# Side work of the attention heads moved between ticks, and one pair of weights turned on TensorE, in a two-layer trunk

## The chip, the cores and the metric

One core of a Trainium2 chip runs the whole program. The metric is the device time of one execution in microseconds (us); before the change it is the median of three runs. The engines are named as the profile names them: PE (TensorE's matmuls), PEld (its weight loads), DVE (VectorE), ACT (ScalarE), POOL (GpSimd) and SP (SyncE, which here only issues DMAs).

## The reference, cut to what matters

Two layers over 256 tokens of width 2048, batch 1, all in float32:

```python
h = rmsnorm(x, norm0); qa,ka,va,iq,ik,iw,qb,kb,vb,gate = split(h @ w_in0)
# A: 10 heads, one shared key/value; an indexer picks 64 causal keys for each query
# B: 6 heads, a mixture of three dilated windows
x = x + (concat(o_a, o_b) * silu(gate)) @ w_out0
h = rmsnorm(x, norm1); qc,kc,vc,qd,kd,vd,fl,gate = split(h @ w_in1)
# C: 8 heads, stick-breaking:
#    w = exp(log_sigmoid(z) + tail), tail = reverse cumulative sum of log_sigmoid(-z)
# D: 8 heads, softmax with forget gates: logits + c[t] - c[s], c = cumsum(log f)
x = x + (concat(o_c, o_d) * silu(gate)) @ w_out1
return rmsnorm(x, norm_f)
```

## The kernel before

**Projections.** The four weight matrices are read as 39 *jobs*, most of them 512 columns wide: 14 for layer 0's input (B0, K, I0, I1, B1 to B3, A0, A2, A4, A6, A8, B4, B5; an A job holds two heads, a *pair*), P0 to P3 for its output, 17 for layer 1's input (C0, F1, G1, C2 to C7, D0 to D7), Q0 to Q3 for its output. A job runs over 16 k-tiles; at each, `project` (L323, L324, L326) issues six matmuls: weights split into a high and a low part (`whi`, `wlo`), tokens likewise, three products for each of two token tiles.

**The split.** Weights arrive as `raw` tiles of four k-tiles (three buffers, DMAs on SP's queue, `load`). `split` halves each: ACT copies `whi` (L282), DVE subtracts `wlo` (L283). It is issued for two k-tiles at a time and runs three of these halves ahead of the matmuls; `whi` and `wlo` have four buffers each.

**Side work.** When a job ends, its head starts as a Python generator. Each k-tile of a full-width job is one *tick* (six matmuls); at each tick `advance` resumes the generators that are due, the oldest first. `yield n` means n ticks later. So the order of every engine's instructions is written out by these numbers: what a head issues at a tick stands in ACT's, DVE's, PE's and SP's queues behind what was issued before and ahead of the next split. A new head starts every 16 ticks, and a head lives 23 to 43 ticks, so two or three heads overlap.

**A head.** A transpose goes by DVE inside 32x32 blocks (`grid`, L428), a store to DRAM (`fard`, L437 or L511) and a read back (L448; in four pieces for the weights, L442); near the end of a layer TensorE does it (`turn`, L400). A C head, in ticks from its start:

- 0: scaled q and k (L866, L867), their `grid`; in `vg1` the value (L487, L490) and the gate u = g * sigmoid(g): ACT's Exp (L877), DVE's add, reciprocal (L882) and product (L887)
- 2 store and 6 read of q and k; 8 `grid` of u, 10 store, 14 read (`gate_late`)
- 10: q and k cut into parts (L408 to L410); 14: scores on PE, z (L936), ACT's Abs, Exp, Ln, Relu (L939 to L942)
- 20: scan (L945), z minus sum (L947), Exp (L948); 22 `grid`, 24 store, 28 read
- 38: the weights cut into parts (`cut`, L477, L478, tiles `ph`, `pl`); 43: matmuls with the value into the one PSUM tile `o` (`weigh_out`, L464 to L466, L531), times the gate (L532), into the parts `yh`, `yl` of the output

A D head runs `softmax_head`: cut of q and k at 10, scores and softmax at 14 (L549, L551), shares (L565) and `grid` at 16, store 18, read 22, cut 26, out 29; its u is turned by `gate_turned` (grid 4, store 6, read 10). D6 and D7 turn on TensorE. A pair of A heads (`heads_a`): rotated q and both gates (L769) at 0, q cut at 12, softmax of the first head at 16, share, `grid` 18, store 20, read 24; the second four ticks later; cuts at 28 and 36 (tiles `pA`, `pB`), out at 39, with the product at L809. All pairs, A8 too, go through DRAM. B4 and B5 turn on TensorE.

All these stores and reads, and the `raw` loads, are issued in order from SP's queue: an issue that waits (for a `grid`, for a store to land, for a free `raw` tile) holds all behind it.

Of the kernel before, what the change touches and what calls it, by code (L numbers as in the profile page):

```python
# [14 lines left out]
P = 128  # L15
# [159 lines left out]
def trunk(ctx, tc, x, xT, g1, w0, wo0, w1, wo1, bf, gf, consts, rope, out):  # L175
# [66 lines left out]
    def load():  # L242
        i = st["load"]
        if i == len(pieces):
            return
        st["load"] += 1
        wd, off, n, w = pieces[i]
        if i < len(FIRST):

            kt = sum(FIRST[:i])  # L250
            raws[i] = home[kt // 8][:, (kt % 8) * w:(kt % 8 + n) * w]
        else:
            raws[i] = wp.tile([P, n * w], F32, name="raw", tag="raw")
        if i == 1 or 3 < i < len(FIRST):
            load_xT(kt)
        nc.sync.dma_start(raws[i], wd[off:off + P * n * w].rearrange("(p f) -> p f", p=P))
        if i in (0, 2):
            load_xT(i)
        if i == len(FIRST) + 1:
            for th in range(NT):  # L260
                for c0, c1 in ((0, D),):
                    nc.sync.dma_start(xs[:, th, c0:c1], x[th * P:(th + 1) * P, c0:c1])
            nc.sync.dma_start(rt.rearrange("p a b -> p (a b)"), rope)
        if i == len(FIRST) + 2:
            nc.sync.dma_start(cons, consts)
# [231 lines left out]
    def gate_turned(u):  # L497
        uT = hp.tile([P, SEQ], F32, name="uT", tag="uT")
        start(far([u], uT, 4, 2, 4))
        return arrived(uT, NT)  # L500

    def gate_late(u, n=NT):

        box = []

        def way():
            yield 8
            t = grid([u])
            d = dr.tile([P, P * n], F32, name="fard", tag=f"fard{n}", bufs=4)
            yield 2  # L510
            nc.sync.dma_start(d, t)  # L511
            yield 4
            uT = hp.tile([P, P * n], F32, name="uT", tag="uT" if n == NT else "rl")
            read_back(uT, d, n)
            box.append(arrived(uT, n))

        start(way())
        return box
# [57 lines left out]
        yield 2 if last else ticks  # L576
        weigh_out(ph, pl, p1, v, uT[0] if isinstance(uT, list) else uT, kt)

    def softmax_head(qk, ticks, nb, v, u, rs, kt, last, near):

        uT = u if last else gate_turned(u)
        qk = yield from qk_turned(qk, ticks, last)
        pr, l = soft(qk, nb() if callable(nb) else nb)
        if not last:
            yield 2
        share(pr, factor(l, rs))
        if near:
            yield 4
            blocks = quarters(turn([pr[:, 0:P], pr[:, P:SEQ], pr[:, SEQ:384]]))
        else:  # L590
            yield from moved(grid([pr]), pr, 2, 4, True)
            yield 4
            blocks = arrived(pr, 3)
        yield from weights_out(blocks, v, uT, kt, last)

# [164 lines left out]
    def heads_a(ps, h):  # L760
        qk = hp.tile([P, 512], F32, name="qk", tag="qk")
        u = hp.tile([P, 2, NT, P], F32, name="u2", tag="u2", bufs=1)
        tgs = {}
        for th in range(NT):
            rotate(qk[:, th * 256:(th + 1) * 256], ps[th][:, 0:256], rt[:, th, 0:P], rt[:, th, 256:384], 2, P)
            tgs[1 - th] = hp.tile([P, 256], F32, name="tg", tag="tg")
            nc.scalar.activation(tgs[1 - th], ps[1 - th][:, 256:512], AF.Tanh, scale=hr0[:, 1 - th:2 - th])
        for th in (1, 0):
            nc.vector.scalar_tensor_tensor(u[:, :, th, :], tgs[th].rearrange("p (a b) -> p a b", a=2), 1.0,  # L769
                                           ps[th][:, 256:512].rearrange("p (a b) -> p a b", a=2),  # L770
                                           op0=OP.add, op1=OP.mult)
        uT = gate_late(u.rearrange("p a b c -> p (a b c)"), 4)
        yield from far([qk], qk, 2, 2, 4)
        yield 4
        q = arrived(qk, 4)
        f = hp.tile([P, 256], F32, name="qqf", tag="qkf", bufs=1)
        hi = hp.tile([P, 256], F32R, name="qqh", tag="qkh", bufs=1)
        lo = hp.tile([P, 256], F32R, name="qql", tag="qkl", bufs=1)
        nc.scalar.activation(quarters(hi), q[:, 2:4], AF.Copy)
        nc.scalar.activation(quarters(f), q[:, 0:2], AF.Copy)  # L780
        nc.vector.tensor_tensor(quarters(lo), q[:, 2:4], quarters(hi).bitcast(F32), op=OP.subtract)
        yield 4
        js = [slice(j * P, (j + 1) * P) for j in range(2)]
        away = []
        for j in range(2):
            pr, l = soft((f[:, js[j]], kA, hi[:, js[j]], lo[:, js[j]], kAh, kAl), nbA)
            yield 2
            share(pr, factor(l, hr0))

            t = hp.tile([P, 512], F32, name="far", tag=("ih2", "il2")[j], bufs=1)[:, 0:384]  # L790
            start(moved(grid([pr], t), t, 2, 4, True))
            away.append(arrived(t, 3))
            yield 2
        yield 4

        ph, pl = (hp.tile([P, 2, SEQ], F32R, name="pA" + n, tag="i" + n, bufs=1) for n in "hl")
        p1h, p1l = (hp.tile([P, 2 * P], F32R, name="pB" + n, tag=t, bufs=1) for n, t in (("h", "y"), ("l", "sp")))
        for j in range(2):
            cut((quarters(ph[:, j, :]), quarters(pl[:, j, :])), away[j][:, 0:2])
            cut((quarters(p1h[:, js[j]]), quarters(p1l[:, js[j]])), away[j][:, 2:3])  # L800
            yield (8, 3)[j]
        uT, = uT
        po = pa.tile([P, 512], F32, name="o", tag="o", bufs=1)
        vh, vl = vAs
        flat = lambda t: t.rearrange("p a b -> p (a b)")
        three_of(po, vh[:, 0], vl[:, 0], flat(ph), flat(pl), True, False)
        o1 = po.rearrange("p (a b c) -> p a b c", a=2, b=2)[:, :, 1, :]
        three_of(o1, vh[:, 1], vl[:, 1], p1h, p1l, False, True)
        nc.vector.tensor_tensor(uT, quarters(po), uT, op=OP.mult)  # L809
        kt = YPOS[f"A{h}"]  # L810
        cut([quarters(flat(t[:, kt:kt + 2, :])) for t in ys], uT)
# [55 lines left out]
            nc.vector.tensor_scalar(qk[:, k], ps[th][:, P:256], r1[:, th:th + 1], None, op0=OP.mult)  # L867
        return qk

    def vg1(ps, o, apart=False, third=False):  # L870

        u = hp.tile([P, SEQ], F32, name="u", tag="u")
        e = hp.tile([P, SEQ], F32, name="e", tag="tg")
        v, upper, lower = values(ps, o, r1, (), third)
        for th in range(NT):
            t = slice(th * P, (th + 1) * P)
            nc.scalar.activation(e[:, t], ps[th][:, o + P:o + 256], AF.Exp, scale=nr1[:, th:th + 1])  # L877
            upper(th)
        if apart:
            yield 1  # L880
        nc.vector.tensor_scalar(e, e, 1.0, 3.0e38, op0=OP.add, op1=OP.min)
        nc.vector.reciprocal(e, e)  # L882
        if apart:
            yield 1
        for th in range(NT):
            t = slice(th * P, (th + 1) * P)
            nc.vector.scalar_tensor_tensor(u[:, t], ps[th][:, o + P:o + 256], r1[:, th:th + 1], e[:, t],  # L887
                                           op0=OP.mult, op1=OP.mult)
        lower()
        return v, u  # L890

    def forget(ps):
# [36 lines left out]

    def stick(qk, ticks, v, u, kt):  # L930

        uT = gate_late(u)
        qk = yield from qk_turned(qk, ticks, 0)
        pZ = scores(qk)
        z = hp.tile([P, 384], F32, name="z", tag="sn")
# [2 lines left out]
        zp = hp.tile([P, 384], F32, name="zp", tag="ih", bufs=1)  # L938
        nc.scalar.activation(sp, z, AF.Abs)  # L939
        nc.scalar.activation(sp, sp, AF.Exp, scale=-1.0)  # L940
        nc.scalar.activation(sp, sp, AF.Ln, bias=1.0)
        nc.scalar.activation(zp, z, AF.Relu)  # L942
        yield 6
        for _, s in BLK:
            nc.vector.tensor_tensor_scan(sp[:, s][:, ::-1], sp[:, s][:, ::-1], zp[:, s][:, ::-1], 0.0,  # L945
                                         op0=OP.add, op1=OP.add)
# [1 line left out]
        nc.scalar.activation(z, z, AF.Exp)  # L948
        yield 2
        yield from moved(grid([z]), z, 2, 4, True)  # L950
        yield 10
        yield from weights_out(arrived(z, 3), v, uT, kt, 0, 5)

    def head_c(ps, h):
        qk = scaled_qk(ps, 0, (0, 3), (1, 2))
        start(moved(grid([qk]), qk, 2, 4))
        v, u = yield from vg1(ps, 256, h == 0, h % 3 == 2)
        yield from stick(qk, 10 if h else 8, v, u, h)

# [12 lines left out]

    def tail(ps, c2):
# [123 lines left out]
```

## Time and profile before

| | |
|---|---|
| median of 3 runs | 898.07 us (895.04 to 900.7) |
| the profiled execution | 896.82 us |
| its span, first to last instruction | 894.7 us |
| PE, PEld busy | 879.1 us (98%), 734.5 us (82%) |
| DVE, ACT, POOL busy | 659.0 us (74%), 475.3 us (53%), 50.2 us (6%) |
| granted TensorE clock, mean | 0.997 of full speed |

Busy times are sums over the profiled execution; a matmul's duration overlaps the next one's, so a busy PE is not a PE at its full rate. The step from one matmul's start to the next one's shows the rate. A row of a timeline shows the start, the duration, the instruction, and in brackets the engine's idle time before it and what ended it. `out<-in` are names of tiles.

### The profile page before, as it was taken

What the parts mean: (1) busy time and instruction counts of PE and PEld (TensorE: products, weight loads), DVE (VectorE), ACT (ScalarE), POOL (GpSimd) and SP (SyncE); (2) the same over time, 40 slices, a digit from 0 to 9 for tenths busy, and PEclk for the clock granted to TensorE, in tenths of its full rate; (3) what the DMA queues carried; (4) which work ended last, traced back from release to release, by engine and by line L of the source; (5) the groups of instructions that cost most, each with busy time, mean ns of one, the idle gap of its engine ahead of it and who ended that gap; (6) DMA issues with size and microseconds to landing.
All of it is one profiled execution on the core that took longest, in us unless ns stands there. A gap on an engine that the chain in (4) does not pass through costs nothing.

```text
span 894.7 us, 12055 instructions
## 1 busy us (share of the span) xinstructions
PE 879.1 (98%) x4185; PEld 734.5 (82%) x4185; DVE 659.0 (74%) x1162; ACT 475.3 (53%) x840; POOL 50.2 (6%) x69
## 2 busy tenths in 40 slices
PE   9999999999999999999999999999999999999996
PEld 6988888888888877888898888888777888888886
DVE  7587888877777777666667777777787777776563
ACT  7644555454454555555455555555555555555440
POOL 0013100000000000000000000000010000001110
PEclk9999999999999999999999999999999999999998
DMA  9887555676777765766486756666685776665542
GB/s 360 316 314 268 209 204 192 209 265 208 258 247 234 228 219 210 277 229 243 146 287 222 254 202 238 217 231 224 231 281 202 268 236 244 236 219 182 192 185 95
DMA packets 89661, 207.59 MB, mean 232 GB/s; under 512 B 32112, under 2 KB 60800, under 8 KB 71424
## 3 DMA queue, kind: packets, MB, share of 16 engines
q1 hardware_dynamic: 88128, 203.52, 64.7%
q0 software_dynamic: 896, 2.12, 0.8%
q10 hardware_dynamic: 576, 1.19, 0.4%
q8 instruction: 33, 0.54, 0.2%
q14 instruction: 28, 0.23, 0.1%
HBM read 185.29 MB, written 21.50 MB: 231 GB/s over the span
## 4 chain that ended last, share of the span: by engine, by line
PE 79%; DVE 8%; DMA 6%; issue 3%; ACT 3%; SPq 1%; POOL 0%; DVEq 0%; POOLq 0%; ACTq 0%
PE pj L323 25%; PE pj L324 25%; PE pj L326 25%; DVE wlo L283 3%; DMA raw<-in_w_out_dram 2%; DMA qk<-fard 2%; ACT whi L282 2%; DMA raw<-in_w_in_dram 1%; DMA fard<-far 1%; DVE far L428 1%; DVE e L882 1%; PE s L538 1%; PE o L531 0%; PE s L465 0%; PE s L466 0%
## 5 line engine op out<-in xcount | busy, mean ns | idle before, releaser
L283 DVE TENSOR_TENSOR wlo<-raw,whi 128x1024 fp32r<-128x1024 f32 (+3 forms) x300 | 352.6, 1189 | 149.7 <-ACT whi L282 148.2
L323 PE MATMUL pj<-whi,xh 128*128 128x512 f32 (+3 forms) x992 | 378.5, 383 | 0.0
L324 PE MATMUL pj<-whi,xl 128*128 128x512 f32 (+3 forms) x992 | 376.4, 381 | 0.0
L282 ACT ACTIVATE whi<-raw 128x1024 fp32r<-128x1024 f32 (+3 forms) x300 | 299.8, 1025 | 123.6 <-PE pj L324 73.4
L326 PE MATMUL pj<-wlo,xh 128*128 128x512 f32 (+3 forms) x992 | 297.3, 381 | 1.9 <-DVE wlo L283 1.8
L326 PEld LDWEIGHTS pj<-wlo,xh 128*128 128x128 f32 x992 | 182.9, 188 | 39.8 <-DVE wlo L283 4.5
L323 PEld LDWEIGHTS pj<-whi,xh 128*128 128x128 f32 x992 | 186.7, 188 | 34.0 <-ACT whi L282 1.3
L324 PEld LDWEIGHTS pj<-whi,xl 128*128 128x128 f32 x992 | 186.6, 188 | 33.0
L323 PE MATMUL pj<-whi,yh 128*128 128x512 f32 (+1 forms) x248 | 95.7, 386 | 0.0
L324 PE MATMUL pj<-whi,yl 128*128 128x512 f32 (+1 forms) x248 | 94.9, 383 | 0.0
L326 PE MATMUL pj<-wlo,yh 128*128 128x512 f32 (+1 forms) x248 | 76.7, 382 | 0.0
L326 PEld LDWEIGHTS pj<-wlo,yh 128*128 128x128 f32 x248 | 46.6, 188 | 9.2
L324 PEld LDWEIGHTS pj<-whi,yl 128*128 128x128 f32 x248 | 46.7, 188 | 8.7
L323 PEld LDWEIGHTS pj<-whi,yh 128*128 128x128 f32 x248 | 46.6, 188 | 8.6
L477 ACT ACTIVATE yh<-uT 128x256 fp32r<-128x256 f32 (+1 forms) x27 | 12.4, 458 | 61.1 <-DVE uT L532 45.2
L551 ACT ACTIVATE sn<-sn,nm 128x128 f32<-128x128 f32 (+1 forms) x48 | 21.5, 449 | 35.2 <-DVE nm L549 35.2
L598 ACT ACTIVATE sq<-xs 128x512 f32<-128x512 f32 x23 | 14.3, 623 | 30.2 <-DVE xs L821 26.5
L882 DVE RECIPROCAL e<-e 128x256 f32<-128x256 f32 x16 | 28.1, 1753 | 0.6
L382 POOL TENSOR_TENSOR qk<-rot,rot 128x256 f32<-128x256 f32 x16 | 11.9, 741 | 230.3 <-ACT sn L551 109.7
L948 ACT ACTIVATE z<-z 128x384 f32<-128x384 f32 x8 | 4.2, 526 | 38.0 <-DVE z L947 38.0
L877 ACT ACTIVATE e<-pj,nr 128x128 f32<-128x128 f32 x32 | 11.8, 367 | 21.9 <-DVE qk L867 21.9
L478 DVE TENSOR_TENSOR yl<-uT,yh 128x256 fp32r<-128x256 f32 (+1 forms) x27 | 12.8, 475 | 14.3 <-ACT yh L477 14.3
(216 smaller groups left out, 715.0 us busy)
## 6 DMA issues: line engine op xcount, KB each, us to landing
raw<-in_w_in_dram SPq DMA_DIRECT2D x108, 1024.0 KB, 6.1
raw<-in_w_out_dram SPq DMA_DIRECT2D x32, 1024.0 KB, 4.9
fard<-far SPq DMA_DIRECT2D x43, 256.0 KB, 2.1
qk<-fard SPq DMA_DIRECT2D x25, 256.0 KB, 5.2
fard<-far SPq DMA_DIRECT2D x28, 192.0 KB, 2.0
raw<-in_w_in_dram SPq DMA_DIRECT2D x4, 672.0 KB, 10.0
fard<-far SPq DMA_DIRECT2D x20, 128.0 KB, 4.6
uT<-fard SPq DMA_DIRECT2D x20, 128.0 KB, 4.2
```

The lines of the kernel that those rows point to most:

```text
L282: nc.scalar.activation(hi, rw, AF.Copy)
L283: nc.vector.tensor_tensor(lo, rw, hi.bitcast(F32), op=OP.subtract)
L323: nc.tensor.matmul(o, a, wh, start=(kt == 0), stop=False)
L324: nc.tensor.matmul(o, b, wh, start=False, stop=False)
L326: nc.tensor.matmul(o, a, wl, start=False, stop=(kt == KT - 1))
L382: nc.gpsimd.tensor_tensor(dst, t1[:, 0:n], t2[:, 0:n], op=OP.add)
L477: nc.scalar.activation(dst[0], src, AF.Copy)
L478: nc.vector.tensor_tensor(dst[1], src, dst[0].bitcast(F32), op=OP.subtract)
L551: nc.scalar.activation(sn[:, s], sn[:, s], AF.Exp, scale=-1.0, bias=nm[:, th:th + 1], accum_out=l[:, th:th + 1])
L598: nc.scalar.activation(j, xs[:, th, c * 512:(c + 1) * 512], AF.Square, accum_out=ss[:, i, th, c:c + 1])
L877: nc.scalar.activation(e[:, t], ps[th][:, o + P:o + 256], AF.Exp, scale=nr1[:, th:th + 1])
L882: nc.vector.reciprocal(e, e)
```

## The change

1. `stick`: after Abs and Exp of z four ticks pass before Ln and Relu, then four (instead of six) to the scan. The weights' `grid`, store and read come two ticks later (24, 26, 30), the cut is at 38 as before.
2. `vg1`: the value's low part first; add and reciprocal two ticks later, the product two ticks after that, now for all C and D heads but D7 (C0 had it with one tick each). The later `yield`s are cut by four, so that q and k are cut at tick 10 as before. C heads' u is turned at the same ticks as before; D heads' u by `gate_late` (grid 8, store 10, read 14).
3. `heads_a`: u is formed at tick 4; the pair's store, read, first cut come two ticks later (22, 26, 30 for the first head; store 26, read 30 for the second), the second cut stays at 36, out at 40. The cut weights get rooms named afresh.
4. The last pair (A8, `near`) turns its weights on TensorE: six `turn` matmuls, no store and read; its cuts are at 21 and 24, out at 27 instead of 39.
5. `softmax_head(behind)`: D0's cut comes four ticks later (30, out 33).
6. `load`: x is read in four DMAs instead of two.

```diff
-                for c0, c1 in ((0, D),):
+                for c0, c1 in ((0, 1024), (1024, D)):
                     nc.sync.dma_start(xs[:, th, c0:c1], x[th * P:(th + 1) * P, c0:c1])
...
-    def gate_late(u, n=NT):
+    def gate_late(u, first=8, n=NT):
...
-            yield 8
+            yield first
             t = grid([u])
...
-        uT = u if last else gate_turned(u)
+        uT = u if last else gate_late(u, 4) if rs is None else gate_turned(u)
...
             yield from moved(grid([pr]), pr, 2, 4, True)
-            yield 4
+            yield 8 if behind else 4
...
 def heads_a
+        start(far([qk], qk, 2, 2, 4))
+        yield 4
         for th in (1, 0):
             nc.vector.scalar_tensor_tensor(u[:, :, th, :], ...
-        uT = gate_late(u.rearrange("p a b c -> p (a b c)"), 4)
-        yield from far([qk], qk, 2, 2, 4)
-        yield 4
+        uT = gate_late(u.rearrange("p a b c -> p (a b c)"), 4, 4)
+        yield 8
...
+        near = h == HA - 2
+        if near:
+            sm = []
+            for j in range(2):
+                sm.append(scored(j))
+                yield 2
+                share(sm[j][0], factor(sm[j][1], hr0))
+            yield 1
+            ph, pl, p1h, p1l = rooms(("ih2", "il2"), ("ph", "pl"))
+            for j in range(2):
+                pr = sm[j][0]
+                turned(j, quarters(turn([pr[:, 0:P], pr[:, P:SEQ], pr[:, SEQ:384]])))
+                yield 3
+        else:
...
-            start(moved(grid([pr], t), t, 2, 4, True))
+                start(moved(grid([pr], t), t, 4, 4, True))
...
-        yield 4
-        for j in range(2):
-            cut(...)
-            yield (8, 3)[j]
+            yield 6
+            ph, pl, p1h, p1l = rooms(("ih", "il"), ("y", "sp"))
+            turned(0, away[0])
+            yield 6
+            turned(1, away[1])
+            yield 4
...
 def vg1
+        lower()
         if apart:
-            yield 1
+            yield 2
         nc.vector.tensor_scalar(e, e, 1.0, 3.0e38, op0=OP.add, op1=OP.min)
         nc.vector.reciprocal(e, e)
         if apart:
-            yield 1
+            yield 2
...
-        lower()
         return v, u
...
 def stick
-        uT = gate_late(u)
+        uT = gate_late(u, 4)
...
         nc.scalar.activation(sp, sp, AF.Exp, scale=-1.0)
+        yield 4
         nc.scalar.activation(sp, sp, AF.Ln, bias=1.0)
         nc.scalar.activation(zp, z, AF.Relu)
-        yield 6
+        yield 4
...
         yield from moved(grid([z]), z, 2, 4, True)
-        yield 10
+        yield 8
...
-        v, u = yield from vg1(ps, 256, h == 0, h % 3 == 2)
-        yield from stick(qk, 10 if h else 8, v, u, h)
+        v, u = yield from vg1(ps, 256, True, h % 3 == 2)
+        yield from stick(qk, 6, v, u, h)
...
-        v, u = yield from vg1(ps, 256, third=h == 0)
-        yield from softmax_head(qk, 10, lambda: biases[h], v, u, None, HC + h, last, h >= HDD - 2)
+        v, u = yield from vg1(ps, 256, not last, h == 0)
+        yield from softmax_head(qk, 6, lambda: biases[h], v, u, None, HC + h, last, h >= HDD - 2, h == 0)
```

## Rows read from the trace of the kernel before

**Rows 1.** The page's first lines: the span, and busy time, share of the span and instructions of each engine.

```profile
span 894.7 us, 12055 instructions
...
PE 879.1 (98%) x4185; PEld 734.5 (82%) x4185; DVE 659.0 (74%) x1162; ACT 475.3 (53%) x840; POOL 50.2 (6%) x69
```

**Rows 2.** Busy time of each engine, with the count of instructions, in windows that reach from a job's first projection matmul to the next job's (columns: window, its length, PE, PEld, DVE, ACT, POOL, granted clock, DMA share, GB/s). In order: jobs D3, C6, C7, D0, D1, D2, then A8, B4 and B5.

```profile
678.09:701.05 22.96, 22.96 (x108) 19.17 (x107) 18.29 (x32) 12.32 (x23) 1.83 (x3) 1.00 0.76 259
...
560.73:584.05 23.32, 23.27 (x107) 19.09 (x106) 17.73 (x26) 13.23 (x25) 0.00 (x0) 1.00 0.66 225
584.05:607.55 23.50, 23.29 (x108) 19.09 (x106) 17.73 (x26) 13.41 (x25) 0.00 (x0) 1.00 0.68 238
607.55:631.03 23.48, 23.27 (x107) 19.08 (x106) 17.97 (x28) 13.19 (x24) 0.72 (x1) 1.00 0.64 214
631.03:655.20 24.17, 23.29 (x107) 19.08 (x106) 18.77 (x31) 13.59 (x25) 1.83 (x3) 1.00 0.67 230
655.20:681.70 26.50, 24.15 (x112) 19.59 (x111) 19.18 (x36) 14.39 (x31) 0.71 (x1) 1.00 0.74 252
254.30:278.30 24.00, 24.00 (x114) 20.08 (x113) 19.28 (x41) 12.44 (x25) 1.49 (x2) 1.00 0.73 235
278.30:303.06 24.76, 24.27 (x114) 20.02 (x113) 18.92 (x42) 12.89 (x25) 1.48 (x2) 1.00 0.73 235
303.06:328.70 25.64, 24.54 (x115) 20.02 (x113) 19.17 (x43) 13.29 (x27) 1.48 (x2) 1.00 0.74 247
```

**Rows 3.** Timeline of PE in job D1, two matmuls in succession at k-tile 6.

```profile
639.87 0.39 PE L324 MATMUL pj<-whi,xl 128*128 128x512 f32 x1
641.14 0.73 PE L326 MATMUL pj<-wlo,xh 128*128 128x512 f32 x2 [0.88 <-DVE wlo L283]
```

**Rows 4.** Timeline of DVE in job C6, from the start of the head before it (C5) to that head's predecessor's scan.

```profile
564.54 0.61 DVE L867 TENSOR_SCALAR qk<-pj,rstd 128x128 f32<-128x128 f32 x2
565.18 0.71 DVE L428 STREAM_TRANSPOSE far<-qk 128x512 f32<-128x512 f32 x1
565.84 0.29 DVE L881 TENSOR_SCALAR e<-e 128x256 f32<-128x256 f32 x1
566.16 1.75 DVE L882 RECIPROCAL e<-e 128x256 f32<-128x256 f32 x1
567.95 0.61 DVE L887 SCALAR_TENSOR_TENSOR u<-pj,rstd,e 128x128 f32<-128x128 f32 x2
568.48 0.34 DVE L490 SCALAR_TENSOR_TENSOR v<-pj,rstd,v 128x128 fp32r<-128x128 f32 x1
568.74 2.35 DVE L283 TENSOR_TENSOR wlo<-raw,whi 128x1024 fp32r<-128x1024 f32 x2
571.00 1.00 DVE L945 TENSOR_TENSOR_SCAN sp<-sp,zp 128x128 f32<-128x128 f32 x2
```

**Rows 5.** Timeline of ACT in the same stretch.

```profile
561.48 0.53 ACT L941 ACTIVATE sp<-sp 128x384 f32<-128x384 f32 x1
561.91 0.51 ACT L942 ACTIVATE zp<-z 128x384 f32<-128x384 f32 x1
...
572.63 0.52 ACT L948 ACTIVATE z<-z 128x384 f32<-128x384 f32 x1 [4.67 <-DVE z L947]
573.06 1.04 ACT L282 ACTIVATE whi<-raw 128x1024 fp32r<-128x1024 f32 x1
```

**Rows 6.** Timeline of PE in job D2: C7's matmuls into `o`, the projection matmul behind them, and, two ticks later, the first of D0's into `o`.

```profile
671.02 0.28 PE L464 MATMUL o<-ph,v 128*128 128x256 f32 x1
...
671.51 0.48 PE L323 MATMUL pj<-whi,xh 128*128 128x512 f32 x1
...
676.35 0.36 PE L464 MATMUL o<-ph,v 128*128 128x256 f32 x1 [1.82 <-DVE uT L532]
```

**Rows 7.** Timeline of PE in jobs B4 and B5: the second matmul of the out of the pairs A4 and A6.

```profile
289.31 0.50 PE L465 MATMUL o<-pAl,vAh 128*128 128x512 f32 x1 [0.49 <-DVE pAl L478]
...
314.94 0.50 PE L465 MATMUL o<-pAl,vAh 128*128 128x512 f32 x1 [1.07 <-DVE pAl L478]
```

**Rows 8.** Timeline of PE in job P0, where B5's head turns its q and k on TensorE and makes its scores.

```profile
335.63 0.44 PE L400 MATMUL tp<-cons,qk 128*128 128x128 f32 x2 [0.72 <-POOL qk L380]
...
339.46 0.49 PE L538 MATMUL s<-qkf 128*128 128x128 f32 x2 [0.30 <-ACT qkf L409]
...
340.57 0.39 PE L465 MATMUL s<-qkl,qkh 128*128 128x256 f32 x1 [0.50 <-DVE qkl L410]
```

**Rows 9.** SP's queue in job B5 (start, time of the issues, what is issued): the read of A8's first weights, and a `raw` load.

```profile
322.49 1.74 SPq L442 DMA_DIRECT2D far<-fard  x4
324.33 0.39 SPq L256 DMA_DIRECT2D raw<-in_w_out_dram  x1
```

**Rows 10.** Timeline of PE in job Q0: D6's three transposes on TensorE and the projection matmuls behind them.

```profile
802.44 0.49 PE L400 MATMUL tp<-cons,sn 128*128 128x128 f32 x3
802.68 0.48 PE L323 MATMUL pj<-whi,yh 128*128 128x512 f32 x1
803.00 0.39 PE L324 MATMUL pj<-whi,yl 128*128 128x512 f32 x1
```

**Rows 11.** SP's queue near the start: the loads of x.

```profile
14.81 0.94 SPq L262 DMA_DIRECT2D xs<-in_x_dram  x2
```

**Rows 12.** The page's DMA issues: the stores of turned weights (count, KB each, median us from issue to landing).

```profile
fard<-far SPq DMA_DIRECT2D x28, 192.0 KB, 2.0
```

More of the change, by code (lines that the diff above doesn't have):

```diff
@@ L577, in weights_out, with softmax_head @@
         weigh_out(ph, pl, p1, v, uT[0] if isinstance(uT, list) else uT, kt)
-    def softmax_head(qk, ticks, nb, v, u, rs, kt, last, near):
-        uT = u if last else gate_turned(u)
+    def softmax_head(qk, ticks, nb, v, u, rs, kt, last, near, behind=False):
+        uT = u if last else gate_late(u, 4) if rs is None else gate_turned(u)
         qk = yield from qk_turned(qk, ticks, last)
@@ L783, in heads_a @@
         js = [slice(j * P, (j + 1) * P) for j in range(2)]
-        away = []
-        for j in range(2):
[L786 to L790, printed above, removed]
-            start(moved(grid([pr], t), t, 2, 4, True))
-            away.append(arrived(t, 3))
-            yield 2
-        yield 4
-        ph, pl = (hp.tile([P, 2, SEQ], F32R, name="pA" + n, tag="i" + n, bufs=1) for n in "hl")
@@ L797, in heads_a, with rooms @@
[L797 to L800, printed above, removed]
-            yield (8, 3)[j]
+        near = h == HA - 2
+        scored = lambda j: soft((f[:, js[j]], kA, hi[:, js[j]], lo[:, js[j]], kAh, kAl), nbA)
+        def rooms(a, b):
+            return ([hp.tile([P, 2, SEQ], F32R, name="pA" + n, tag=t, bufs=1) for n, t in zip("hl", a)]
+                    + [hp.tile([P, 2 * P], F32R, name="pB" + n, tag=t, bufs=1) for n, t in zip("hl", b)])
@@ new lines, in turned @@
+        def turned(j, pt):
+            cut((quarters(ph[:, j, :]), quarters(pl[:, j, :])), pt[:, 0:2])
+            cut((quarters(p1h[:, js[j]]), quarters(p1l[:, js[j]])), pt[:, 2:3])
+        if near:
[11 more added lines that the diff above has]
+        else:
+            away = []
+            for j in range(2):
+                pr, l = scored(j)
+                yield 2
+                share(pr, factor(l, hr0))
+                t = hp.tile([P, 512], F32, name="far", tag=("ih2", "il2")[j], bufs=1)[:, 0:384]
+                start(moved(grid([pr], t), t, 4, 4, True))
+                away.append(arrived(t, 3))
+                yield 2
[5 more added lines that the diff above has]
+            yield 4
@@ L868, in scaled_qk, with vg1 @@
         return qk
-    def vg1(ps, o, apart=False, third=False):
+    def vg1(ps, o, apart=True, third=False):
         u = hp.tile([P, SEQ], F32, name="u", tag="u")
@@ L878, in vg1 @@
             upper(th)
+        lower()
         if apart:
-            yield 1
+            yield 2
         nc.vector.tensor_scalar(e, e, 1.0, 3.0e38, op0=OP.add, op1=OP.min)
@@ L883, in vg1 @@
         if apart:
-            yield 1
+            yield 2
         for th in range(NT):
@@ L956, in head_c @@
         start(moved(grid([qk]), qk, 2, 4))
-        v, u = yield from vg1(ps, 256, h == 0, h % 3 == 2)
-        yield from stick(qk, 10 if h else 8, v, u, h)
+        v, u = yield from vg1(ps, 256, True, h % 3 == 2)
+        yield from stick(qk, 6, v, u, h)
     def head_cf(ps, qk):
         v, u = yield from vg1(ps, 0)
-        yield from stick(qk, 10, v, u, 1)
+        yield from stick(qk, 6, v, u, 1)
     def head_d(ps, h):
```

## The prediction, made before the changed kernel was run

> **What bounds the kernel now.** The page comes first: PE is busy 98% of the span, DVE 74%, ACT 53% [rows 1]. That says that PE sets the end, not that it runs at its full rate, for a busy matmul can stand in the array while the next one waits. So the second view is a table by job: windows from a job's first projection matmul to the next job's. The reader is to see that the windows differ although the jobs are alike. D3 takes 22.96 us, PE is busy all of it at clock 1.00, and D4 to D6 repeat that length; this is a slot in which PE waits for nothing. C6, C7, D0, D1 and D2 hold the same projections and take 23.32, 23.50, 23.48, 24.17 and 26.50 [rows 2]. A8 with its pair's extra matmuls takes 24.00 without a wait, B4 and B5 with as many matmuls 24.76 and 25.64 [rows 2]. Only this excess can be won by moving side work: the matmuls themselves stay.
>
> The third view, PE's timeline, tells what the excess waits for. In D1 the low product of k-tile 6 stands 1.27 us behind the one before it, 0.88 of it idle until DVE's `wlo` [rows 3]. DVE's own timeline shows why `wlo` is late: at a head's start it works off scaled k, `grid`, add, reciprocal, product and the value's low part, from 564.54 to 568.74, before it comes to the split [rows 4]. In D2 the wait is another: D0's matmuls into the single tile `o` wait 1.82 for DVE's product on C7's `o`, two ticks earlier [rows 6]. In B4 and B5 the outs of pairs A4 and A6 wait 0.49 and 1.07 for the second head's low part [rows 7]. In P0 PE waits 0.72, 0.30 and 0.50 for B5's rotated and cut q and k [rows 8]. Behind this lies SP's queue: a `raw` load at 324.33 is issued only after the four reads of A8's weights, which took the queue from 322.49 [rows 9].
>
> **The change, part by part.**
>
> *`vg1` and `stick` (the wlo waits).* Excess over 22.96: 0.36 (C6) + 0.54 (C7) + 0.52 (D0) + 1.21 (D1) = 2.63. In D2 it is 3.54; there two outs fall into one slot, and an out costs PE 0.49 (671.02 to 671.51) [rows 6], so 3.05 is waiting: 1.82 at `o`, the other 1.23 mostly `wlo`. The change takes add, reciprocal and product (0.29 + 1.75 + 0.61 = 2.65) out of the cluster ahead of k-tile 6's `wlo` [rows 4]; the longest of these waits in the slots is 1.21, so it goes with a margin of over 1 us. What is late next? Now 0.29 + 1.75 = 2.04 stands ahead of k-tile 8's `wlo`. Before, both `wlo` ended at 571.09; after, by the same durations, 568.74 - 2.65 + 1.18 + 2.04 + 1.18 = 570.49: no later. On ACT, Ln and Relu (0.53 + 0.51) [rows 5] no longer stand ahead of a split at tick 14, but at tick 18, when a new head's Exps have just gone; same work, smaller lump. z's Exp, for which ACT now idles 4.67 ahead of k-tile 10's `whi` [rows 5], comes two ticks later, ahead of k-tile 12's; DVE is then less behind, so that wait shrinks. I take the whole of it: -2.63 and -1.23. Bounds: 0, if the lump only moves, and -3.86.
>
> *D0 four ticks later (`behind`).* Its matmuls come six ticks after C7's instead of two. Two ticks are 2 x 22.96/16 = 2.9 us, and they missed by 1.82 [rows 2, 6], so six are enough: -1.82. What hides the delay is that D0's output is read only in Q0, five slots on.
>
> *The pairs.* B4 0.76 + B5 1.64 over A8's 24.00 [rows 2]. Out at 40 leaves four ticks instead of three behind the second cut: 1.4 us more against waits of 0.49 and 1.07 [rows 7]. Stores come two ticks later, so that they are issued when their `grid` is done and don't hold the `raw` loads in SP's queue. -2.40; bounds 0 and -2.40.
>
> *The last pair on TensorE.* Removed from SP: two stores and eight reads (a set of four takes 1.74 of the queue [rows 9]), on which `raw` loads of P0 wait. Added on PE: six transposes. Three took 802.44 to 803.00 with the first matmul behind them [rows 10], of which a matmul's own step is about 0.23 (a slot of 22.96 over some 96 projections and 12 smaller matmuls): 0.33, twice 0.66. ACT and DVE do the same cuts, from PSUM. The waits in P0, 0.72 + 0.30 + 0.50 = 1.52 [rows 8], should shrink since A8's second cut no longer stands ahead of B5's q and k on ACT, and `raw` is earlier; I take half, -0.76, for the rotation there is not touched. Bounds 0 and -1.52.
> For a 128x128 transpose the Trainium skill (TensorE: Matmul & The Clock Gate, Part 4: PE-mode transpose) has about 275 ns in a kernel's context. By that the six would cost 1.65 and the sum below would be 1.0 smaller; the trace here has 0.33 for three.
>
> *The rest.* Gates of D heads are stored and read four ticks later, z's store and reads two ticks later: as many DMAs as before, on the same queue. z's store now meets the gate's store (tick 10 of the next head), its four reads the gate's read (14), and the `raw` loads of tick 16 stand behind them. Weights are read at 30 and cut at 38: eight ticks, 11.5 us. x in four pieces adds two issues, 0.47 each [rows 11], where SP then waits for `raw` buffers: 0, at most +0.94.
>
> *New waits* that no row shows: 0 to 1.82 (the longest wait that PE's rows have [rows 6]); I put +1.0, nearer the middle, since the ends of three heads are newly interleaved.
>
> Sum: -2.63 - 1.23 - 1.82 - 2.40 - 0.76 + 0.66 + 1.0 = -7.2. The profiled execution took 896.82 (span 894.7 and 2.1 around it), 1.25 below the median: it would be 889.6, and the median 898.07 - 7.2 = **890.9**.
>
> **Rivals.**
> 1. *The lump moves.* DVE's work in a slot stays 17.7 to 19.2 us [rows 2]; `wlo` is late at k-tile 8 or 12 instead of 6, and the 3.86 comes back: -3.3, 894.7. For it: the slack is not seen in the rows. Against it: the count above, 570.49 against 571.09.
> 2. *The last pair makes PE wait.* PE takes its queue in order, and each turn can wait for DVE as B5's do (0.72 [rows 8], twice 1.44); A6's and A8's outs now come three ticks apart in the one `o` and can wait 1.82 as in rows 6. With the pairs' 2.40 + 0.76 lost as well: -7.2 + 1.44 + 1.82 + 3.16 = -0.8, 897.3. For it: B4 and B5 are the slots where DVE is busiest but D2. Against it: three ticks are 4.3 us, a miss of 1.82 at 2.9 us would fit in.
> 3. *Slower: z's reads hold `raw`.* The four reads at tick 30 wait on SP for a store issued four ticks before; if it lands later than that (5.7 us), the `raw` load of tick 16 is late in every C slot, as in B5, whose excess is 1.64 [rows 2, 9]: eight C heads x 1.64 = 13.1, C and D win nothing, the pairs' -2.40 - 0.76 + 0.66 stay: +10.6, 908.7. Against it: such a store lands in 2.0 us in the median [rows 12], and the distance of four ticks is the same as before.
> 4. *Nothing new waits*, and all 1.52 in P0 goes: -2.63 - 3.05 - 2.40 - 1.52 + 0.66 = -8.9, 889.2. More than this the waits don't hold.
> 5. *There is more room than slots show.* If PE's steps in a slot of 22.96 themselves waited on side work, more could be won: its weight loads are busy 19.17 of it [rows 2], which leaves 3.8 a slot. Nothing is idle in D3 and four slots agree in length to 0.01, so I give it 1 in 100.
> By the rule of the Trainium skill (Perfetto Trace Analysis, Identifying the Most-Contended Engine) headroom is judged by the weight loads' share, here 82%, and not by matmul time; the trace speaks against it as a measure for this stream.
>
> **How the numbers follow.** Forecast 0.55 (own range 889 to 893), rival 1 0.18, rival 2 0.13, rival 3 0.06, rivals 4 and 5 together 0.08. The range 887.5 to 897.5 holds the forecast, rivals 1 and 4 and half of rival 2; outside are rival 3, the other half, and a few hundredths below. One per cent is 9.0 us, about what a measurement of this kernel can tell from no change (its three runs lie 5.7 apart): faster than 889.1 takes rival 4 or 5, and half of rival 4 lies above it by its spread, so 0.09 with the forecast's edge; slower than 907.1 is rival 3, 0.06; the rest, 0.85, is within 1%.
>
> **What would show it.** In a table by job: C6 to D1 back at 22.96 (wlo part); D2 near 22.96 with no wait at `o` and D3 near 23.45, since D0's out moves into it (behind); B4 near 24.0; in B5 twice three transposes and a second pair's out, taken over from P0, with no wait behind them (last pair). The forecast is wrong where the table shows the excess in other slots of C and D, a `turn` or `o` matmul in B5 with a long idle before it, or `raw` loads later than now in SP's queue.

## The result, and the profile after

The changed kernel takes 888.09 us (median of 4 runs, 887.99 to 888.68) beside 896.81 (895.04 to 900.7) of the kernel before, run with it: the medians are 8.7 us apart, and the ratio measured from the runs is 0.9892, 95% interval 0.9859 to 0.9926. By the ratio that is just past the one per cent (9.0 us) which the prediction called no change, with a chance of 0.85; by the medians just short of it, and the interval holds both. The time is inside the prediction's range and 2.8 below its number; 1.3 of the 2.8 is that the median of before, shown as 898.07, came out at 896.81 here. The profiled executions give the finer figure: span 894.7 before, 886.1 after, -8.6. The page's first lines, after:

```profile
span 886.1 us, 12056 instructions
...
PE 876.8 (99%) x4191; PEld 736.3 (83%) x4191; DVE 656.7 (74%) x1160; ACT 474.6 (54%) x840; POOL 51.1 (6%) x69
```

PE's busy time fell by 2.3 us only [rows 1]; it is the 8.6 in the span that tells. The table by job, after, has the columns of rows 2; in order B4, B5, P0, C2, C6 (C7, left out, is as long), D0, D1, D2, D3:

```profile
278.27:302.27 24.00, 24.00 (x114) 20.08 (x113) 19.40 (x41) 12.67 (x25) 1.49 (x2) 1.00 0.76 250
302.27:328.06 25.79, 25.79 (x126) 21.61 (x125) 19.76 (x44) 14.17 (x30) 1.48 (x2) 1.00 0.58 198
328.06:353.04 24.98, 24.98 (x126) 20.96 (x125) 17.81 (x39) 15.14 (x30) 1.48 (x2) 1.00 0.50 175
463.74:486.78 23.04, 23.04 (x109) 19.11 (x108) 16.82 (x23) 13.34 (x21) 0.94 (x2) 1.00 0.76 269
555.70:578.67 22.97, 22.97 (x108) 19.17 (x107) 17.61 (x26) 12.97 (x25) 0.00 (x0) 1.00 0.67 233
...
601.64:624.62 22.98, 22.98 (x108) 19.18 (x107) 17.59 (x27) 13.04 (x24) 0.72 (x1) 1.00 0.63 208
624.62:647.66 23.04, 23.04 (x108) 19.23 (x107) 17.38 (x29) 13.28 (x24) 1.83 (x3) 1.00 0.70 225
647.66:671.52 23.86, 23.74 (x108) 18.94 (x107) 19.50 (x37) 13.36 (x29) 0.71 (x1) 1.00 0.92 299
671.52:695.11 23.59, 23.59 (x113) 19.75 (x112) 18.37 (x34) 13.77 (x27) 1.84 (x3) 1.00 0.74 247
```

The same view of the kernel before for the two jobs that rows 2 lack, P0 and C2:

```profile
328.70:357.56 28.86, 27.17 (x131) 21.75 (x130) 20.89 (x45) 16.96 (x34) 1.46 (x2) 1.00 0.57 206
468.26:491.81 23.55, 23.24 (x109) 18.91 (x107) 16.78 (x23) 14.09 (x23) 0.54 (x1) 1.00 0.67 233
```

Against rows 2, C6 to D1 fall from 94.47 to 91.96 us, D2 + D3 from 49.46 to 47.45, B4 + B5 + P0 from 79.26 to 74.77, C2 from 23.55 to 23.04: together -9.5. The rest, +0.9, lies in none of these: +0.3 in the first two jobs, -0.2 ahead of the first projection matmul and +0.8 behind the last one (7.36 before, 8.17 after; the cause stays open). C2's -0.51 should not be put down to the change: e3 and e4 below, whose layer 1 is that of the changed kernel, take 23.51 and 23.56 there.

So the slots moved about as foretold, except that the pairs and P0 gave 4.49 where 2.50 was summed. That the reasons held is a further question, and the experiments say no for two of them.

### The profile page after: what moved, and what is told of

Its sections match the earlier page's. It is cut to its first block, busy times and chain, and to the rows that moved or that the text cites. A ratio compares the mean times of both kernels' runs of the same rounds, so it can differ in the third digit from the quotient of the medians.

```text
span 886.1 us, 12056 instructions
## 1 busy us (share of the span) xinstructions
PE 876.8 (99%) x4191; PEld 736.3 (83%) x4191; DVE 656.7 (74%) x1160; ACT 474.6 (54%) x840; POOL 51.1 (6%) x69
## 4 chain that ended last, share of the span: by engine, by line
PE 94%; issue 2%; DVE 2%; ACT 1%; POOL 0%; POOLq 0%; DVEq 0%; ACTq 0%
PE pj L323 29%; PE pj L324 29%; PE pj L326 29%; DVE wlo L283 1%; PE s L538 1%; ACT whi L282 1%; PE s L465 1%; PE o L531 1%; PE s L464 1%; PE s L466 1%; PE o L464 0%; PE o L465 0%; PE o L466 0%; PE s L1041 0%; PE tp L400 0%
```

## The experiments

In the diffs a minus line is the kernel that the text names as its base. The sums that the verdicts rest on are slot lengths as in the tables above.

### The pairs

**e1**, the changed kernel with A8 through DRAM like the other pairs:

```diff
-        near = h == HA - 2
+        near = False
```

> The changed kernel with its last pair A8 through DRAM again, at the new ticks (read at 26 and 30, cuts at 30 and 36). Slots B4 + B5 + P0 took 79.26 us before and 74.77 after the change. Theory 1 (the stores and reads of A8 hold raw loads in SP's queue, and this made the waits of P0): the sum goes back up by 2.5 to 4, to 77.3 to 78.8, with raw loads of P0 issued late behind far<-fard reads. Theory 3 (the pairs' later stores did it): the sum falls by the six transposes' 0.66, to about 74.1.

It took 886.77 us (886.62 to 887.17), ratio 0.9909 (0.988 to 0.9939), and B4 + B5 + P0 took 74.07. The ratios do not tell it from the changed kernel; the slots do. PE waits nowhere in these three slots in either kernel, and e1 has six matmuls fewer there: turning the last pair on TensorE is a loss of 0.70 us, the price of its six transposes, and the pairs' other ticks are the gain. (Another 0.46 lies behind the last projection matmul, 7.71 beside 8.17.)

**e2**, the kernel before with the last pair's turn alone (its `turned` on TensorE as in the change, all other ticks old).

> The kernel before with nothing but A8's weights turned on TensorE. Theory 1: P0 falls by about 3.5 with one out less in it and few waits, B5 rises by an out and the transposes less what its own wait of A6 gives back; B4 stays at 24.76 since its wait is A4's. Sum of B4, B5, P0 75 to 76.5. Theory 3: sum 78.5 to 80, waits in P0 stay. Layer 1 as before: C6 to D2 at 23.32, 23.50, 23.48, 24.17, 26.50.

895.77 us (10 runs), ratio 1.0007 (0.9988 to 1.0025). P0 fell to 25.02 us, but B5 rose to 28.80, and the sum stayed, 79.23. That is theory 3's sum, but P0's waits did not stay, as it had said; B5 has them now. A row of PE's timeline in B5 shows a new wait, for the softmax of A8 on DVE:

```profile
308.15 0.49 PE L538 MATMUL s<-kA,qqf 128*128 128x128 f32 x2 [1.31 <-DVE nm L549]
```

**e3**, the changed kernel with A8's DRAM path beside its turn; the `grid`, store and reads are work whose result nothing uses:

```diff
                 yield 2
                 share(sm[j][0], factor(sm[j][1], hr0))
+                t = (u.rearrange("p a b c -> p (a b c)"), qk)[j][:, 0:384]
+                start(moved(grid([sm[j][0]], t), t, 4, 4, True))
             yield 1
```

> The changed kernel, A8's weights turned on TensorE, but their two grids, two stores and eight reads are issued as well, at the ticks of the DRAM path, into tiles that nothing reads. Theory 1 (queue): most of e1's loss comes though nothing waits for the data: sum of B4, B5, P0 76.5 to 78.5. Theory 2 (A8's second cut waits in ACT's order for its late landing, ahead of B5's q and k): the sum stays within 0.5 of 74.77.

888.92 us (ratio 0.9929, 0.9907 to 0.9952), sum 75.65, 0.88 more than the changed kernel and in neither theory's range. A8's DMAs cost something, far from the 4.5 that the slots gained.

**e4**, the changed kernel with the first four pairs at their old ticks:

```diff
-                start(moved(grid([pr], t), t, 4, 4, True))
+                start(moved(grid([pr], t), t, 2, 4, True))
...
-            yield 6
+            yield 4
...
-            yield 6
+            yield 8
...
-            yield 4
+            yield 3
```

(and u formed at tick 0 again).

> The changed kernel with the first four pairs at their old ticks (gates formed at 0, stores at 20 and 24, cuts at 28 and 36, out at 39), A8 on TensorE as in the change. Theory 1: B4 goes back to 24.76 (its wait of 0.49 in A4's out), B5 gets A6's wait back in part (0.5 to 1.1), P0 stays near 25.0: sum 75.5 to 76.8. Theory 3: P0 gets its waits back as well, sum 77 to 79.

891.86 us (10 runs), ratio 0.9961 (0.994 to 0.9983), sum 78.63: nearly all of the gain is gone. The sum is theory 3's, the place is not: P0 stays at 25.03, and B5 takes 28.91.

**e8, e9, e10**: which of the pairs' ticks it is. Base is e1 (store at 22 and 26, read at 26 and 30, u at tick 4).

```diff
e8
-                start(moved(grid([pr], t), t, 4, 4, True))
+                start(moved(grid([pr], t), t, 2, 6, True))
e9
-                start(moved(grid([pr], t), t, 4, 4, True))
+                start(moved(grid([pr], t), t, 4, 2, True))
e10
-        start(far([qk], qk, 2, 2, 4))
-        yield 4
...
-        uT = gate_late(u.rearrange("p a b c -> p (a b c)"), 4, 4)
-        yield 8
+        uT = gate_late(u.rearrange("p a b c -> p (a b c)"), 8, 4)
+        yield from far([qk], qk, 2, 2, 4)
+        yield 4
```

> The kernel with the last pair through DRAM (e1), but with the pairs' stores two ticks earlier, as in the kernel before (20 and 24); the reads stay at 26 and 30, so six ticks lie between store and read. Theory (a read that waits for its store to land holds the raw loads behind it on SP; more ticks between them are as good as a later store): SP waits under 6 us for stores to land in the windows of A6 to P0, the windows B4, B5 and P0 sum to 74.0 to 74.6 us, time 886.6 to 887.4. Rival (the store must be issued at a place where no raw load stands just ahead of it; issued at 20 and 24 it lands some 8 us later and the reads wait all the same): SP waits over 15 us there, the sum is 76 to 79 us, time 889 to 892.

> The kernel with the last pair through DRAM (e1), the pairs' stores late (22, 26) as there, but their reads two ticks earlier, at 24 and 28: two ticks between store and read. Theory (what holds the raw loads is a read that waits in SP's queue for its own store; two ticks are 3 us): SP's waits of reads for stores in 230 to 337 us grow from 5.5 to 10 to 20 us, the sum B4 + B5 + P0 from 74.07 to 74.5 to 77 us, time 887 to 890. Rival (the place of the store ahead of a raw load is what counts): waits below 7 us, sum within 0.4 of 74.07, time 886.6 to 887.2.

> The kernel with the last pair through DRAM (e1), but the pairs' gates are formed at the pair's start again (u at tick 0 instead of 4). Theory (the stores' and reads' ticks do it, the gates' place does not): B4 + B5 + P0 within 0.5 us of 74.07, time 886.6 to 887.3. Rival (u formed ahead of the split at a pair's start makes wlo late, as the prediction held for the heads of layer 1): the sum is 75 to 77 us, time 888 to 890.

e8 888.56 us (ratio 0.991, 0.9876 to 0.9945), sum 75.12. e9 888.79 (0.9911, 0.9888 to 0.9935), sum 76.61. e10 887.77 (0.9899, 0.9872 to 0.9925), sum 74.08. SP's waits at the reads of weights (L442) in the stretch 230 to 337 us (total, times, longest), in order the kernel before, the changed kernel, e8, e9, e10:

```profile
SPq L442 <- DMA fard<-far: 39.2, 8, 5.6
```
```profile
SPq L442 <- DMA fard<-far: 3.9, 3, 1.9
```
```profile
SPq L442 <- DMA fard<-far: 3.7, 2, 3.1
```
```profile
SPq L442 <- DMA fard<-far: 33.1, 8, 6.2
```
```profile
SPq L442 <- DMA fard<-far: 3.8, 4, 1.5
```

The two with long waits, before and e9, have sums of 79.26 and 76.61; those with short ones lie between 74.08 and 75.12. The ratios of e1, e8, e9 and e10 (0.9899 to 0.9911) are too close to rank them, so what follows rests on the slots of one execution each. P0 goes with SP's waits: 28.86 before, and in e9, e8 and e1

```profile
326.38:354.79 28.41, 26.98 (x132) 21.88 (x131) 20.17 (x43) 16.98 (x34) 1.48 (x2) 1.00 0.59 200
```
```profile
326.53:353.64 27.11, 26.73 (x131) 21.82 (x130) 20.82 (x46) 17.16 (x36) 1.47 (x2) 1.00 0.50 167
```
```profile
326.22:352.28 26.06, 26.06 (x132) 21.88 (x132) 19.58 (x43) 16.02 (x33) 1.48 (x2) 1.00 0.49 168
```

B4 and B5 do not go with them. With the long waits of e9 they take 24.17 and 24.03, with the short ones of e8 24.01 and 24.00, where before had 24.76 and 25.64. What e8 and e9 share with e1 are the ticks of the cuts and of the out; no run moved these alone, so that they removed the waits in B4 and B5 is likely, not shown. Nor is the excess of these two slots fixed: e12 below, with the layer 0 of the kernel before, has 24.05 and 24.82 (and P0 at 28.84).

The order in SP's queue shows how its waits hold the weights. Before (first fence) a pair's read follows its store with no `raw` load between, after (second) with one, and in e9 (third) again with none:

```profile
263.38 0.45 SPq L437 DMA_DIRECT2D fard<-far  x1
266.49 0.37 SPq L448 DMA_DIRECT2D qk<-fard  x1
271.32 1.74 SPq L442 DMA_DIRECT2D far<-fard  x4
273.11 0.43 SPq L256 DMA_DIRECT2D raw<-in_w_in_dram  x1
```
```profile
261.91 0.46 SPq L437 DMA_DIRECT2D fard<-far  x1
263.18 0.37 SPq L448 DMA_DIRECT2D qk<-fard  x1
266.14 0.33 SPq L256 DMA_DIRECT2D raw<-in_w_in_dram  x1
268.46 1.75 SPq L442 DMA_DIRECT2D far<-fard  x4
```
```profile
262.64 0.49 SPq L437 DMA_DIRECT2D fard<-far  x1
266.65 0.37 SPq L448 DMA_DIRECT2D qk<-fard  x1
270.80 1.74 SPq L442 DMA_DIRECT2D far<-fard  x4
272.58 0.43 SPq L256 DMA_DIRECT2D raw<-in_w_in_dram  x1
```

From store to read it is 7.9, 6.6 and 8.2 us; what differs is whether the next weights are under way meanwhile. In the changed kernel that `raw` load goes out at 266.14, before at 273.11. Of the 2.80 that P0 loses in e1, the later read alone brings 1.75 (e8) and the later store alone 0.45 (e9); the gate's place does nothing (e10, whose sum is as its theory said and whose time 0.5 above its range). e9's waits, 33.1, are longer than its theory's 10 to 20. e8's waits are short, as its theory said, but its sum and time lie above that theory's ranges: why its P0 is 27.11 where e1's is 26.06 stays open.

### The heads of layer 1

**e5**, the changed kernel without `behind`:

```diff
-            yield 8 if behind else 4
+            yield 4
```

> The changed kernel, but D0's weights are cut at tick 26 and D0's out comes at 29 as in the kernel before. Theory (the wait at the single tile o is what D0's four ticks remove): PE waits again at D0's first matmul into o, by 1.5 to 1.9 us as in the 1.82 of before, D2 takes 25.5 to 26.3 us instead of 23.86 and D3 22.96 instead of 23.59, together +1.2 to +1.9 us, time 889.3 to 890. Rival (with C7's weights and its gate in other places DVE's product is early anyway, the four ticks do nothing): the wait is under 0.5 us, D2 and D3 together within 0.4 us of 47.45, time 887.9 to 888.4.

889.5 us (889.01 to 890.03), ratio 0.9918 (0.9885 to 0.9951). D2 takes 25.76 and D3 22.96, together 1.27 more, and the wait is back at `o`, shorter than in rows 6:

```profile
669.00 0.35 PE L464 MATMUL o<-ph,v 128*128 128x256 f32 x1 [1.07 <-DVE uT L532]
```

**e6** and **e7** undo one half each of what was done to the heads: e6 forms the gates at the head's start, e7 leaves z's four steps together. Base is the changed kernel.

```diff
e6, vg1 (later yields made up: cut of q and k and grid of u at their ticks)
-        lower()
         if apart:
             yield 2
...
+        lower()
         return v, u
...
-        v, u = yield from vg1(ps, 256, True, h % 3 == 2)
+        v, u = yield from vg1(ps, 256, False, h % 3 == 2)
e7, stick
         nc.scalar.activation(sp, sp, AF.Exp, scale=-1.0)
-        yield 4
         nc.scalar.activation(sp, sp, AF.Ln, bias=1.0)
         nc.scalar.activation(zp, z, AF.Relu)
-        yield 4
+        yield 8
```

> The changed kernel, but add, reciprocal and product of every head's gate stand at the head's start again, ahead of the value's low part (z's four steps stay two and two). Theory (the gate's three steps on DVE are what made wlo late, prediction's first step): the waits of C6 to D1 come back, their four windows sum to 94.0 to 94.6 us (before 94.47, changed kernel 91.96), D2 gains some tenths, time 890.2 to 891. Rival (ACT's four steps on z in one lump did it, by a late whi): the four windows stay within 0.4 us of 91.96, time 888 to 888.5.

> The changed kernel, but Abs, Exp, Ln and Relu of z stand together at tick 14 again (scan at 22, weights as in the changed kernel). Theory (gate): the four windows of C6 to D1 stay within 0.4 us of 91.96, time 888 to 888.5. Rival (z's lump on ACT): the waits come back, the four windows sum to 93.5 to 94.6 us, time 889.6 to 890.8.

Both came out the other way, and e7 lies beyond its rival's ranges too. e6: 887.39 us (887.17 to 888.15), ratio 0.9896 (0.9863 to 0.9928); C6 to D1 take 91.89, D2 22.97, D3 23.80, so D2 + D3 are 0.68 *shorter* than with the gates spread. F1, the slot behind C0, takes 12.25 there instead of 11.57, so that the span, 886.0, is no shorter. e7: 896.75 us (10 runs), ratio 0.9987 (0.9968 to 1.0005), and C6 to D1 take 98.33, longer than before the change; C2 (25.15) and C5 (23.38) lose another 2.5. The windows of e7 for C6 and D0:

```profile
558.38:582.63 24.25, 24.17 (x108) 18.92 (x107) 17.61 (x27) 13.39 (x24) 0.00 (x0) 1.00 0.69 223
...
606.88:631.80 24.92, 24.21 (x108) 18.94 (x107) 18.28 (x29) 13.39 (x24) 0.72 (x1) 1.00 0.64 203
```

ACT's and DVE's timelines explain C5 to D1; why C2 is so long stays open. ACT's Abs of z in two heads in succession, before, after, e6 and e7:

```profile
560.36 0.53 ACT L939 ACTIVATE sp<-z 128x384 f32<-128x384 f32 x1 [1.76 <-DVE z L936]
583.85 0.53 ACT L939 ACTIVATE sp<-z 128x384 f32<-128x384 f32 x1 [1.76 <-DVE z L936]
```
```profile
554.83 0.53 ACT L965 ACTIVATE sp<-z 128x384 f32<-128x384 f32 x1 [1.76 <-DVE z L962]
...
568.35 0.52 ACT L975 ACTIVATE z<-z 128x384 f32<-128x384 f32 x1 [4.63 <-DVE z L974]
...
578.11 0.53 ACT L965 ACTIVATE sp<-z 128x384 f32<-128x384 f32 x1 [1.76 <-DVE z L962]
```
```profile
555.13 0.53 ACT L965 ACTIVATE sp<-z 128x384 f32<-128x384 f32 x1 [2.21 <-DVE z L962]
...
567.90 0.53 ACT L975 ACTIVATE z<-z 128x384 f32<-128x384 f32 x1 [3.87 <-DVE z L974]
...
578.10 0.53 ACT L965 ACTIVATE sp<-z 128x384 f32<-128x384 f32 x1 [2.21 <-DVE z L962]
```
```profile
560.00 0.53 ACT L965 ACTIVATE sp<-z 128x384 f32<-128x384 f32 x1 [1.76 <-DVE z L962]
...
574.50 0.52 ACT L974 ACTIVATE z<-z 128x384 f32<-128x384 f32 x1 [5.46 <-DVE z L973]
...
584.25 0.53 ACT L965 ACTIVATE sp<-z 128x384 f32<-128x384 f32 x1 [1.76 <-DVE z L962]
```

From Abs to Abs: 23.49 before, 23.28 after, 22.97 in e6, 24.25 in e7, beside PE's 22.97. ACT and DVE work as one chain: Abs waits for DVE's z, `whi` stands behind Abs and its like on ACT, `wlo` waits for `whi`, the next head's q and k stand behind `wlo`, ACT's Exp waits for these, and so on round to the next z. Neither engine is busy all the time (DVE 17.6 us, ACT 13.0 of a slot), but each waits for the other in turn, and the chain had a period of its own. Where it is longer than PE's, each head uses up the difference of the split's lead. Before, that is 0.52 a head: Abs starts 21.55, 22.09 and 22.61 us behind the slot's first matmul in C3, C4 and C5, and C6 is the first of them to take more than 22.97. With 0.31 after, it is D1 (by 0.07) and then D2; with 1.28 in e7, C5. In e6 PE sets the pace: ACT waits 0.45 longer for each z (2.21 beside 1.76).

From Abs to z's Exp it is 13.52 us after, 12.77 in e6, 14.50 in e7; from there to the next Abs 9.76, 10.20 (with the 0.45) and 9.75. So Ln and Relu ahead of the split cost 0.98 a head, and spreading the gate *costs* 0.75. DVE's rows say where the latter comes from, `wlo` behind the value's low part after (first fence) and the same place in e6 (second):

```profile
560.53 1.23 DVE L283 TENSOR_TENSOR wlo<-raw,whi 128x1024 fp32r<-128x1024 f32 x1 [0.92 <-ACT whi L282]
561.67 0.29 DVE L908 TENSOR_SCALAR e<-e 128x256 f32<-128x256 f32 x1
```
```profile
559.96 1.75 DVE L908 RECIPROCAL e<-e 128x256 f32<-128x256 f32 x1
...
562.28 0.34 DVE L490 SCALAR_TENSOR_TENSOR v<-pj,rstd,v 128x128 fp32r<-128x128 f32 x1
562.53 3.48 DVE L283 TENSOR_TENSOR wlo<-raw,whi 128x1024 fp32r<-128x1024 f32 x3
```

The gate's three steps had filled the time in which DVE has no `whi` to work on; moved away, they leave 0.92 idle there and come back where DVE was needed. The two terms join the kernels: 23.28 + 0.98 - 0.75 = 23.51, and before had 23.49.

**e12**, the kernel before with z's part alone:

```diff
         nc.scalar.activation(sp, sp, AF.Exp, scale=-1.0)
+        yield 4
         nc.scalar.activation(sp, sp, AF.Ln, bias=1.0)
         nc.scalar.activation(zp, z, AF.Relu)
-        yield 6
+        yield 4
...
-        yield 10
+        yield 8
```

> The kernel before with one part of the change alone: Ln and Relu of z four ticks behind Abs and Exp, the scan at 22 and the weights' grid, store and read two ticks later; gates, pairs, D0 and loads of x as before. Theory now (the heads' work runs as a chain back and forth between ACT and DVE; from one head's Abs to the next it took 23.50 us in the kernel before, more than PE's 22.97, and Ln and Relu ahead of the split are 0.97 us of it, so it falls to about 22.97 or less, and the gate needs no change): the four windows C6 to D1 sum to 91.8 to 92.2 us (before 94.47), Abs to Abs 22.97, D2 loses its wlo part but keeps a wait at o, -2.5 to -4 us, 892.8 to 894.5 beside a before of 896.8. Rival (it takes gate and z together): the windows stay above 93.3 us, time within 1 us of before.

893.06 us (9 runs; the profiled one, 890.66, was the fastest), ratio 0.9948 (0.9933 to 0.9963); C6 to D1 sum to 91.89, Abs to Abs is 22.97, D2 takes 24.90. Three lines do all that was won in C6 to D1.

**e14**, the best by these findings: e1 with the gates of C2 to C7 and of the D heads as in e6.

> The kernel with the last pair through DRAM (e1), and the gates of C2 to C7 and of the D heads formed at the head's start again (e6; C0 and C1 keep the spread). Theory (both changes are losses by themselves, 0.70 us for the six transposes, and 0.68 in D2 and D3, where the spread gate's chain of 23.29 us a head has eaten the split's slack): C2 to D1 without a wait, D2 22.97 and D3 23.80 us, B4 + B5 + P0 74.1 us, time 886.0 to 886.8, 1.3 below the changed kernel. Rival (the pairs' slots or D2 depend on the gate's place otherwise): D2 and D3 above 47.3 us or the sum of B4 to P0 above 75, time 887 to 888.3.

886.12 us (5 runs, 885.85 to 887.38), ratio 0.9882 (0.9863 to 0.9902). F1 is back at 11.57 (C0 keeps the spread), no slot from C3 to D2 takes over 22.98, D2 + D3 take 46.56, B4 + B5 + P0 74.08. The median is 2.0 below the changed kernel's; by slots 0.89 + 0.69 = 1.58 are shown, and 0.47 lies behind the last projection matmul, as in e1. D2 of e14, with D0's delay and no wait:

```profile
646.92:669.89 22.97, 22.97 (x107) 19.18 (x106) 18.15 (x32) 12.68 (x26) 0.71 (x1) 1.00 0.87 279
```

The load of x in four pieces was not tried alone. The first two jobs, where it stands, take 38.1 us in the changed kernel, and 37.8, 38.2 and 38.0 in before, e2 and e12, which read x in two: no cost of it is seen.

## Why the prediction was right and wrong, step by step

- **C6 to D1, -2.63: the size was right (-2.51), the cause was wrong.** The step of the prediction that failed is "The change takes add, reciprocal and product (...) out of the cluster ahead of k-tile 6's `wlo`". DVE was seen to work without a gap there [rows 4] and that was taken for the cause of the late `wlo`. It was late with the whole chain; the gate merely filled a wait for ACT. What helps is what the text passed over as "same work, smaller lump", Ln and Relu: 0.98 a head (e7), alone enough (e12). That the size came is luck: the change happened to move these as well. The gate's spread is a loss of 0.75 a head (e6), hidden until the lead is gone.
- **D2's `wlo`, -1.23, and `o`, -1.82: -2.01 of 3.05 came.** `behind` is worth 1.27 (e5), less than 1.82, since the wait that it removes had shrunk to 1.07 through the other moves. The 0.9 that stays in D2 is the spread gate's chain: e14 has 2.90 of the 3.05.
- **Pairs, last pair and P0, -2.40 + 0.66 - 0.76 = -2.50: it was -4.49, and the term that was mis-sized is P0's.** B4 and B5 gave 2.39 in e1, against -2.40, and the transposes cost 0.70, against 0.66. P0 fell by 2.80 in e1, against -0.76, and this alone is more than the time lies past the sum. The step that failed there is the pricing by the waits of rows 8 (1.52, "I take half"). They were too small a bound even in whole: idle time was 1.69 (28.86 less 27.17 busy), and the other 1.1 stood in matmuls that count as busy. The prediction also tied P0 to A8's cut and A8's DMAs. Removing both (e2) clears P0 but puts the time into B5; moving the pairs' ticks, with A8 still through DRAM, clears both (e1), and P0 follows SP's waits at the reads of weights (e8, e9). For B4 and B5 its reason, the later out, fits e9, but was not tried alone.
- **New waits, +1.0: none came** but the 0.9 in D2. C2's -0.51 is no part of the account, since the same code has 23.51 in e3.
- **Rivals.** That the lump moves (1) was nearer the truth as a mechanism than its chance said: in e6 against the changed kernel it is DVE's moved gate that makes D2 wait. The last pair making PE wait (2) is what e2 shows, with 1.31 in B5, and e4, with 1.4; in the changed kernel, where the other pairs' ticks are moved as well, PE waits nowhere in B5. Two of its readings were wrong, without weight in the sum: the turn's 0.72 in rows 8 was a wait for POOL's rotated q and k, not for DVE, and A8, without a wait, has more DVE work (19.28) than B4, B5 and D2 [rows 2]. z's reads holding `raw` (3) did not happen: C3 to C5 kept 22.97. The sum without new waits (4), -8.9, was nearest to the span's -8.6, but by other terms: P0 gave more than its 1.52 and D2 less than its 3.05. That the waits don't hold more is wrong: e14, which pays no transposes (0.66), gains 2.58 + 2.90 + 5.18 = 10.7 in slots.

## What to carry to other kernels

When two helper engines hand work back and forth, measure the period of their chain from one round's instruction to the same one in the next, and compare it with the main engine's slot: it can be the bound with neither engine busy, and then an instruction counts only if it lies on the chain, while one that fills a wait costs nothing and should stay. A place in the slot that moves back by the same amount each round is the sign, rounds before the first wait. In a DMA queue issued in order, put an independent load between a store and the read that waits for it (P0 here: 28.41 without, 26.06 with).

## What the runs showed of the hardware that was not expected

A wait of PE can cost more than itself. In the profile of e2, PE idles 1.89 us ahead of D0's first matmul into `o`, as it did for 1.82 in rows 6. There the granted clock stayed at 1.00 [rows 2]. Here, just after PE had gone on, it fell to 0.50, the lower of its two levels (1.2 GHz), and steps between 512-wide matmuls were 0.43 us instead of 0.24 until shortly before 681. PE's timeline and a window of e2:

```profile
676.58 0.36 PE L464 MATMUL o<-ph,v 128*128 128x256 f32 x1 [1.89 <-DVE uT L532]
...
678.00 0.63 PE L324 MATMUL pj<-whi,xl 128*128 128x512 f32 x1
678.43 0.63 PE L323 MATMUL pj<-whi,xh 128*128 128x512 f32 x1
...
681.23 0.40 PE L323 MATMUL pj<-whi,xh 128*128 128x512 f32 x1
681.47 0.39 PE L324 MATMUL pj<-whi,xl 128*128 128x512 f32 x1
```
```profile
677.00:680.00 3.00, 3.00 (x10) 2.52 (x10) 2.00 (x4) 1.25 (x2) 0.00 (x0) 0.50 0.55 115
```

D2 took 28.14 us there, against 26.50. That one execution has such a drop and another has not goes with the spread of the runs, 5.7 us in the kernel before and 0.7 in the changed one, in part. Of 48 runs of the kernel before that stand beside the experiments, the 12 with a mean granted clock of 0.996 or less have a median of 898.67 us, the other 36 one of 896.24. But those 36 still lie between 891.24 and 901.31. Nor does it take the wait at `o`: e4 has none in D2, and its slowest run, 897.60 where the median is 891.86, has the lowest clock of its ten (0.993).

The store at 263.38 before, just behind a `raw` load issued at 262.96, let its read go only at 271.32, 7.9 us later, where such stores land in 2.0 in the median [rows 12]. Whether the load ahead makes it late is not shown.
